# Two-phase 31-tap convolution with three half-length filters, two parts per tile, in a DeltaNet/Conformer layer

## The chip, the cores and the metric

The program runs on one core of one Trainium2 chip. The metric is the device time of one execution, in microseconds (us). The engines are named as the profile names them: PE (TensorE matmul), PEld (its weight load), DVE (VectorE), ACT (ScalarE), POOL (GpSimd), SP (SyncE, which here only issues DMAs). Each engine takes its instructions in the order in which they were written into its queue; they wait for each other through semaphores.

## The reference

One layer over 128 context and 2048 latent tokens of width 1024, in float32:

```python
h = rmsnorm(x, g_pre_mix) * (1.0 + scale_m) + shift_m
proj = h @ w_in
qkv, z, ab, glu = jnp.split(proj, [3 * D_A, 4 * D_A, 4 * D_A + 4 * N_HEADS_A], axis=-1)
qkv = jax.nn.silu(dwconv1d(qkv, conv_qkv))          # 5 taps
...                                                  # gated DeltaNet on q, k, v; z gates its output o
glu_a, glu_b = jnp.split(glu, 2, axis=-1)
u = glu_a * jax.nn.sigmoid(glu_b)
u = dwconv1d(u, conv_cf) + b_conv_cf                 # 31 taps, depthwise, 512 channels
u = jax.nn.silu(layernorm(u, ln_cf_g, ln_cf_b))
mix = jnp.concatenate([o, u], axis=-1) @ w_out
x = x + gate_m * rmsnorm(mix, g_post_mix)
...                                                  # gated MLP with a 3x3 convolution in its gate branch
```

`dwconv1d` pads with zeros on both sides; context and latent tokens are convolved separately.

## The kernel before

The program has four stages: the projections with everything that hangs on them (to about 775 us), the DeltaNet chains (to about 1100), the output projection `mix` (to about 1313), and the MLP. The change lies in the first, and by one edit in the third.

**Stage 1.** The products with `w_in` are 24 jobs in a fixed order on PE. A job multiplies 128 columns of `w_in` with all 2176 tokens, in five token blocks (512, 512, 512, 320, 320), as three fp32r products (high and low halves of both sides; L361 to L363), 120 products in all. The order of the jobs that matter here is: glu0, ab (the small decay and beta projection), k1, z0, k0, glu1, z1, glu2, k2, z2, glu3, k3, z3, q0, v1, q1, v0, v3, v2, q2, q3. A glu job computes two projections, 240 products.

- `do_glu(m, ...)`: ACT takes a sigmoid in PSUM (L385), copies the other half into the big buffer `ub` (L390), DVE multiplies (L391). `ub` holds 128 channels and, along its length, 2048 latent and 128 context tokens with zeros between them.
- `do_cf(m, ub, half)`: the 31-tap convolution of tile m, in two token halves of 1024 and 1167 columns. `conv` makes the first tap on ACT (L372) and the other 30 on DVE, one SCALAR_TENSOR_TENSOR each, in place in `acc` (L375). The result is stored to `d_uc` in DRAM (L399).
- `do_conv5`: the 5-tap convolutions of q, k and v (one tap on ACT, four on DVE, the same lines), a Silu (L417) and what follows: for k small products of keys with keys on PE (`pkk`, L446), copied by ACT into `ar` and stored to `d_a` (L448, L449); for q and k the norms (`pqs`, L456, L460); for v transposes (`pt`, L434).
- `do_scalars`: decay and beta of each token: a row of constants `rb` is loaded (L562), DVE and ACT compute from it and from `abT` (L570 to L598), PE sums with six small products (L600 to L602).
- LayerNorm of the convolution's output: `d_uc` is read back, transposed on PE (`ptl`, L534), its statistics taken on DVE (L535), and later applied.

The big buffers A, B and C (`bigA`, `bigB`, `bigC` in the rows) carry `ub` and the inputs of the 5-tap convolutions in turn, B also the temporaries of `do_scalars`, later the winit and inversion work. The pool `ac` has two accumulators, `sm` four buffers for its shared tag "sm", among them `ar` and the rows `gr` that `do_scalars` stores. The order on every engine is decided when the program is built, by a scheduler that plays the program on a timeline of its own costs; `high_priority` pulls the evacuations of PSUM ahead.

**Stage 3.** `mix_in` loads the 128 tokens of a chunk (`mx`, 8 groups of 128 columns: 0 to 3 are o, 4 to 7 are u), splits them into a high and a low half (`mH` on ACT, L1133; `mL` on POOL, L1134), and PE multiplies them with the halves of `w_out`.

Of the kernel before, what the change touches and what calls it, by code (L numbers as in the profile page):

```python
# [47 lines left out]
def hybrid_step_kernel(ctx, tc, x, wmod, pv, rows, win, wab, wout, wup, wdown, s0, cst,  # L48
# [34 lines left out]
    def pvs(n):  # L83
        a, b = PV[n]
        return pvt[:, a:b]
# [165 lines left out]
    with ExitStack() as s1:  # L251
# [23 lines left out]
        def load_w(m):  # L275
            wt = wp.tile([P, KD, P], F32, name="wt", tag="ws", bufs=1)
            nc.sync.dma_start(wt[:], win[m])
            wr = wp.tile([P, 2, KD, P], F32R, name="wr", tag="wr")
            with tc.high_priority():
                nc.scalar.copy(wr[:, 0], wt[:])  # L280
                nc.gpsimd.tensor_tensor(wr[:, 1], wt[:], wr[:, 0].bitcast(F32), ALU.subtract)
            return wr
# [88 lines left out]
        def conv(dst, src, o, n, w, taps, bias=None):  # L371
            nc.scalar.activation(dst, src[:, o:o + n], AF.Identity, scale=w[:, 0:1],  # L372
                                 bias=0.0 if bias is None else bias)
            for t in range(1, taps):
                nc.vector.scalar_tensor_tensor(dst, src[:, o + t:o + t + n], w[:, t:t + 1], dst, ALU.mult, ALU.add)  # L375

        def do_glu(m, sl, w=None):
            ub = slot(sl, [P, 2224])
            for a, b in ((0, 15), (2063, 2078), (2206, 2221)):
                nc.gpsimd.memset(ub[:, a:b], 0.0)  # L380
            wb, wa = w or (load_w(20 + m), load_w(16 + m))
            for bi in range(len(BLOCKS)):
                s, n, pb = mm_block(wb, bi)
                with tc.high_priority():
                    nc.scalar.activation(pb[:, 0:n], pb[:, 0:n], AF.Sigmoid)  # L385
                s, n, ps = mm_block(wa, bi)
                with tc.high_priority():
                    for a, ln, off, pr in pieces(s, n):
                        o = (2078 if pr else 15) + off
                        nc.scalar.copy(ub[:, o:o + ln], ps[:, a:a + ln])  # L390
                        nc.vector.tensor_tensor(ub[:, o:o + ln], ub[:, o:o + ln], pb[:, a:a + ln], ALU.mult)  # L391
            return ub

        def do_cf(m, ub, half):
            acc = ac.tile([P, 1168], F32, name="acc", tag="acc")
            w = pvs("ccf")[:, 31 * m:31 * m + 31]
            n = 1167 if half else 1024
            conv(acc[:, 0:n], ub, 1024 * half, n, w, 31, pvs("bcf")[:, m:m + 1])
            nc.sync.dma_start(d_uc[8 * half:8 * half + 8, :, m, :].rearrange("c p t -> p c t"),  # L399
                              acc[:, 0:1024].rearrange("p (c t) -> p c t", t=P))  # L400
            if half:
                nc.sync.dma_start(d_uc[16, :, m, :], acc[:, 1039:1167])

        def do_conv5(m, sl, post):
            cb = slot(sl, [P, 2224])
            for a, b in ((0, 2), (2050, 2052), (2180, 2182)):
                nc.gpsimd.memset(cb[:, a:b], 0.0)
            for s, n, ps in project(m):
                with tc.high_priority():
                    for a, ln, off, pr in pieces(s, n):  # L410
                        o = (2052 if pr else 2) + off
                        nc.scalar.copy(cb[:, o:o + ln], ps[:, a:a + ln])  # L412
            for half in range(2):
                acc = ac.tile([P, 1168], F32, name="acc", tag="acc")
                n = 1154 if half else 1024
                conv(acc[:, 0:n], cb, 1024 * half, n, pvs("cqkv")[:, 5 * m:5 * m + 5], 5)
                nc.scalar.activation(acc[:, 0:n], acc[:, 0:n], AF.Silu)  # L417
                post(acc, half, cb)
# [139 lines left out]
            nc.sync.dma_start(d_mix[c, :, 4:8, :], uv)  # L558

        def do_scalars(tt, abT):  # L560
            rb = sm.tile([P, 16], F32, name="rb", tag="rb", bufs=1)
            nc.sync.dma_start(rb[:], rows.to_broadcast([P, 16]))  # L562
            N16 = [P, NT, 16]
            trs = tt[:, 1428:1940].rearrange("p (a t) -> p a t", t=P)
            nc.sync.dma_start(trs, cst[:, 1:5, :])
# [20 lines left out]
            nc.vector.tensor_tensor(t3, t3, t4, ALU.add)  # L586
            nc.vector.tensor_scalar(t0, t0, 0.0, None, ALU.max)
            nc.vector.tensor_tensor(t3, t3, t0, ALU.add)
            ea = sm.tile([P, 8], F32, name="ea", tag="ea", bufs=1)
            nc.scalar.activation(ea[:], rb[:, 0:8], AF.Exp)  # L590
            nc.vector.tensor_scalar(ea[:], ea[:], -1.0, None, ALU.mult)
            NTH = NT * H
            for d in range(2):
                fl = lambda t: t[:, d].rearrange("p c h -> p (c h)")
# [133 lines left out]

        def inv(b, eng):
            invs[b] = invert(b, eng, ltb[:, 0:1056], prod,  # L730
                             lambda: ac.tile([P, 1168], F32, name="xo", tag="acc")[:, 0:1024])
            run(invs[b], 32)

        def inv_end(b):
# [365 lines left out]
    with ExitStack() as s3:  # L1100
# [9 lines left out]
        def mix_in(c):  # L1110
            on = wi.tile([P, H, P], F32, name="on3", tag="on3")
            nc.sync.dma_start(on[:], d_o[c].rearrange("p (h t) -> p h t", h=H))
            zt = wi.tile([P, H, P], F32, name="zt", tag="zt")
            nc.sync.dma_start(zt[:], d_z[c])
            mx = wi.tile([P, KD, P], F32, name="mx", tag="mx")
            nc.sync.dma_start(mx[:, 4:8], d_mix[c, :, 4:8])
            sc = s3p.tile([P, H], F32, name="sc", tag="sc", bufs=2)
            for h in range(H):
                junk = s3p.tile([P, P], BF16, name="junk0", tag="junk0", bufs=4)
                nc.scalar.activation(junk[:], on[:, h], AF.Square, accum_out=sc[:, h:h + 1])  # L1120
            nc.vector.tensor_tensor(sc[:], sc[:], rq2[:, c], ALU.mult)
            last_a = nc.scalar.activation(sc[:], sc[:], AF.Sqrt, scale=1.0 / P, bias=epsb[:]).ins
            nc.vector.reciprocal(sc[:], sc[:])
            last_v = nc.vector.tensor_tensor(sc[:], sc[:], rq[:, c], ALU.mult).ins
            nc.gpsimd.tensor_tensor(on[:], on[:], sc[:].unsqueeze(2).to_broadcast([P, H, P]), ALU.mult)
            po = ptr.tile([P, H, P], F32, name="pto", tag="tr")
            for h in range(H):
                nc.tensor.transpose(po[:, h], on[:, h], ident[:])
            f = lambda t: t.rearrange("p h i -> p (h i)")
            nc.vector.scalar_tensor_tensor(f(mx[:, 0:4]), f(po[:]), pvs("gon"), f(zt[:]), ALU.mult, ALU.mult)  # L1130
            mH = wh.tile([P, KD, P], F32R, name="mH", tag="mH", bufs=2)
            mL = wi.tile([P, KD, P], F32R, name="mL", tag="mL", bufs=2)
            nc.scalar.copy(mH[:], mx[:])  # L1133
            nc.gpsimd.tensor_tensor(mL[:], mx[:], mH[:].bitcast(F32), ALU.subtract)  # L1134
            return mH, mL, last_a, last_v

        def mix_mm(c, mH, mL):
# [78 lines left out]
    if True:  # L1216
# [7 lines left out]
        def taps(j):  # L1224
            return pvf[:, 9 * j:9 * j + 9], pvf[:, 198 + j:199 + j]
# [395 lines left out]
```

## Time and profile before

| | |
|---|---|
| median of 3 runs | 2793.51 us (2789.07 to 2797.16) |
| the profiled execution's own time | 2791.89 us |
| its span in the profile | 2790.1 us |
| mean granted clock of PE over the span | 0.972 |

The profile is of one execution. Its span runs from the first to the last instruction; 1.8 us of the time lie outside it. PE is busy 2654.8 us of the span, DVE 1907.2. A share of the whole span is a mean over four stages with different limits, so the rows below are taken by stage. [...]

### The profile page before, as it was taken

The numbers are of one execution on the slowest core, as the hardware profiler recorded it, in microseconds if no ns is written. First come the engines' busy times: TensorE is split into PE (matmuls) and PEld (weight loads), VectorE is DVE, ScalarE is ACT, GpSimd is POOL, SyncE is SP. The second block draws the span as 40 slices with busy tenths as digits, with TensorE's granted clock in tenths as the row PEclk, the third lists the DMA queues.
The fourth block names the chain that finished last, engine by engine and source line by source line (L and its number), as shares of the span: only waits on it lengthen the run. The fifth ranks groups of instructions, "written<-read, shape, count | busy, mean of one in ns | idle before, by whom it ended". The sixth has DMA issues, their size and how long they took to land.

```text
span 2790.1 us, 41624 instructions
## 1 busy us (share of the span) xinstructions
PE 2654.8 (95%) x15309; PEld 2237.8 (80%) x15309; DVE 1907.2 (68%) x2840; ACT 1153.1 (41%) x2421; POOL 789.9 (28%) x851
## 2 busy tenths in 40 slices
PE   7999999979888998999899999999999999999998
PEld 4888888767778887888788888888888878888887
DVE  3898999885657785444687777887888873225343
ACT  5423132355656666666544444432222232224221
POOL 2211011166335683222666666500000000000000
PEclk9999999989969999999999999999999999999999
DMA  7024531576597565665777777888777754236453
GB/s 275 20 72 119 151 109 43 104 190 134 154 279 195 141 227 207 219 231 184 256 278 266 265 271 262 279 263 255 235 232 222 230 184 134 94 104 211 165 173 119
DMA packets 426712, 526.79 MB, mean 189 GB/s; under 512 B 144790, under 2 KB 301964, under 8 KB 426252
## 3 DMA queue, kind: packets, MB, share of 16 engines
q1 hardware_dynamic: 406380, 506.30, 57.5%
q10 hardware_dynamic: 20128, 17.83, 1.9%
q8 instruction: 121, 1.98, 0.3%
q14 instruction: 83, 0.68, 0.1%
HBM read 342.13 MB, written 181.90 MB: 188 GB/s over the span
## 4 chain that ended last, share of the span: by engine, by line
PE 61%; DMA 5%; DVE 4%; ACT 3%; SPq 3%; POOL 2%; issue 2%; ACTq 0%; DVEq 0%; POOLq 0%
PE ps L1318 10%; PE ps L1320 10%; PE ps L1319 10%; PE ps L1147 7%; PE ps L1486 6%; PE ps L1484 6%; PE ps L1485 6%; PE psc L1232 2%; SPq L166 1%; DVE dm L819 1%; PE p L938 1%; PE p L945 1%; DMA dm<-d_g 1%; DMA d_mix<-bigB 1%; PE p L957 1%
## 5 line engine op out<-in xcount | busy, mean ns | idle before, releaser
L1377 DVE SCALAR_TENSOR_TENSOR pa<-gb,pvf,pa 128x512 f32<-128x512 f32 (+1 forms) x704 | 491.0, 733 | 65.3 <-ACT pa L1375 62.5
L1318 PE MATMUL ps<-T,wr 128*128 128x512 f32 x1232 | 480.5, 391 | 0.1
L1319 PE MATMUL ps<-T,wr 128*128 128x512 f32 x1232 | 479.9, 389 | 0.0
L1320 PE MATMUL ps<-T,wr 128*128 128x512 f32 x1232 | 479.0, 390 | 0.6 <-POOL wr L1246 0.6
L361 PE MATMUL ps<-hH,wr 128*128 128x512 f32 (+1 forms) x960 | 349.7, 369 | 6.6 <-ACT bigA L412 3.8
L362 PE MATMUL ps<-hL,wr 128*128 128x512 f32 (+1 forms) x960 | 352.4, 367 | 0.0
L363 PE MATMUL ps<-hH,wr 128*128 128x512 f32 (+1 forms) x960 | 350.6, 366 | 0.0
L1484 PE MATMUL ps<-wd,yr 128*128 128x512 f32 x748 | 292.5, 391 | 6.1 <-ACT yr L1480 5.5
L1486 PE MATMUL ps<-wd,yr 128*128 128x512 f32 x748 | 292.1, 391 | 0.4 <-DVE yr L1481 0.4
L1485 PE MATMUL ps<-wd,yr 128*128 128x512 f32 x748 | 292.1, 391 | 0.0
L1318 PEld LDWEIGHTS ps<-T,wr 128*128 128x128 f32 x1232 | 231.4, 188 | 49.2 <-issue 0.8
L1320 PEld LDWEIGHTS ps<-T,wr 128*128 128x128 f32 x1232 | 231.4, 188 | 49.1 <-POOL wr L1246 1.1
L1319 PEld LDWEIGHTS ps<-T,wr 128*128 128x128 f32 x1232 | 231.4, 188 | 47.4
L375 DVE SCALAR_TENSOR_TENSOR acc<-bigA,pvt,acc 128x1024 f32<-128x1024 f32 (+2 forms) x168 | 252.3, 1502 | 13.2 <-ACT acc L372 9.2
L361 PEld LDWEIGHTS ps<-hH,wr 128*128 128x128 f32 x960 | 184.0, 193 | 33.5 <-ACT bigA L412 4.2
L1481 DVE TENSOR_TENSOR yr<-yt,yr 128x1408 fp32r<-128x1408 f32 x68 | 110.5, 1625 | 143.4 <-ACT yr L1480 143.3
L363 PEld LDWEIGHTS ps<-hH,wr 128*128 128x128 f32 x960 | 185.4, 193 | 25.4 <-issue 3.0
L362 PEld LDWEIGHTS ps<-hL,wr 128*128 128x128 f32 x960 | 185.3, 193 | 24.0 <-issue 1.6
L1351 POOL TENSOR_TENSOR up<-up,x 128x512 f32<-128x512 f32 x44 | 57.3, 1302 | 413.2 <-ACT pa L1383 217.9
L375 DVE SCALAR_TENSOR_TENSOR acc<-bigC,pvt,acc 128x1024 f32<-128x1024 f32 (+2 forms) x108 | 156.6, 1461 | 24.9 <-DMA bigB<-d_uc 15.5
L1484 PEld LDWEIGHTS ps<-wd,yr 128*128 128x128 f32 x748 | 141.0, 188 | 36.6 <-ACT yr L1480 6.5
L1486 PEld LDWEIGHTS ps<-wd,yr 128*128 128x128 f32 x748 | 141.0, 188 | 30.7 <-DVE yr L1481 1.4
(360 smaller groups left out, 4571.2 us busy)
## 6 DMA issues: line engine op xcount, KB each, us to landing
d_w<-wr SPq DMA_DIRECT2D x154, 512.0 KB
wr<-d_w SPq DMA_DIRECT2D x154, 512.0 KB
yt<-d_y SPq DMA_DIRECT2D x68, 704.0 KB
raw<-in_wup_dram SPq DMA_DIRECT2D x60, 512.0 KB
xt<-in_x_dram SPq DMA_DIRECT2D x34, 512.0 KB
wmt<-in_wmod_dram SPq DMA_DIRECT2D x24, 512.0 KB
wt<-in_win_dram SPq DMA_DIRECT2D x24, 512.0 KB
wmt<-in_wmod_dram SPq DMA_DIRECT2D x48, 256.0 KB
```

The source lines that it names most:

```text
L361: nc.tensor.matmul(ps[:, 0:n], wr[:, 0, k], hH[bi][:, k], start=(k == 0), stop=False)
L362: nc.tensor.matmul(ps[:, 0:n], wr[:, 0, k], hL[bi][:, k], start=False, stop=False)
L363: nc.tensor.matmul(ps[:, 0:n], wr[:, 1, k], hH[bi][:, k], start=False, stop=(k == KD - 1))
L375: nc.vector.scalar_tensor_tensor(dst, src[:, o + t:o + t + n], w[:, t:t + 1], dst, ALU.mult, ALU.add)
L1147: nc.tensor.matmul(pss[hf][:], a[:, k], w[k][:, 512 * hf:512 * hf + 512], start=(w is woH and a is mH and k == KD - 1), stop=(w is woL and ...
L1318: nc.tensor.matmul(ps[:], h, T[i][:, 0, k], start=(first and k == 0), stop=False, skip_group_check=True)
L1319: nc.tensor.matmul(ps[:], h, T[i][:, 1, k], start=False, stop=False, skip_group_check=True)
L1320: nc.tensor.matmul(ps[:], l, T[i][:, 0, k], start=False, stop=(k == HK - 1), skip_group_check=True)
L1377: nc.vector.scalar_tensor_tensor(rows(a), src, w[:, t:t + 1], rows(a), ALU.mult, ALU.add)
L1484: nc.tensor.matmul(ps[:], yr[:, 0, i], wd[:, 0], start=(q == 0 and i == 0), stop=False)
L1485: nc.tensor.matmul(ps[:], yr[:, 0, i], wd[:, 1], start=False, stop=False)
L1486: nc.tensor.matmul(ps[:], yr[:, 1, i], wd[:, 0], start=False, stop=(q == 1 and i == HN - 1))
```

## The change

The convolution is done by phases. With e the even and o the odd tokens, an even output is A(e) + B(o) and an odd output is D(e + o) - A(e shifted) - B(o), where A has the 16 even taps, B the 15 odd taps and D the 16 sums of neighbouring taps. So three filters of half length replace two phases of full length.

- `do_glu` writes `ub` de-interleaved: one half of the buffer for each parity. ACT and DVE read PSUM with a stride of two elements for it (L393, L394 in the changed file).
- `do_cf` works in two parts of 512 and 584 tokens per parity. ACT makes two first taps (L412, L413), DVE 15 taps of A and 14 of B, which take turns, then the sum of the parities in place (L418), the two outputs' start (L420, L421), and 16 steps of D (L422, and 15 in L399): 48 instructions of half length where 30 of full length stood. The D output stays in `ub`, and each part is stored as two blocks with runs of 64 elements (256 bytes) where runs of 128 (512 bytes) stood. POOL saves and restores 15 columns around the sum of the first part (L417, L425).
- Within each chunk of 128 tokens the order in `d_uc` is now all even, then all odd tokens. `mix_in` undoes it: `mH` and `mL` are made in two pieces each, the second with a strided read of `mx`.
- `wc`, the sums of taps, is a new small buffer. To keep the memory, `rb` leaves its own buffer and takes one of the four of the tag "sm", and `ea` becomes a part of it. The accumulators have 1169 columns for 1168; the weight buffers stay two.

```diff
@@ -376,8 +376,9 @@
         def do_glu(m, sl, w=None):
             ub = slot(sl, [P, 2224])
-            for a, b in ((0, 15), (2063, 2078), (2206, 2221)):
+            for a, b in ((0, 7), (1031, 1039), (1103, 1119), (2143, 2151), (2215, 2224)):
+            uv = ub.rearrange("p (h i) -> p h i", h=2)
...
                     for a, ln, off, pr in pieces(s, n):
-                        o = (2078 if pr else 15) + off
-                        nc.scalar.copy(ub[:, o:o + ln], ps[:, a:a + ln])
-                        nc.vector.tensor_tensor(ub[:, o:o + ln], ub[:, o:o + ln], pb[:, a:a + ln], ALU.mult)
+                        o = (1039 if pr else 7) + off // 2
+                        u = uv[:, :, o:o + ln // 2]
+                        ev = lambda t: t[:, a:a + ln].rearrange("p (i h) -> p h i", h=2)
+                        nc.scalar.copy(u, ev(ps))
+                        nc.vector.tensor_tensor(u, u, ev(pb), ALU.mult)
+        def taps(dst, src, w, n, t0):
+            for t in range(t0, n):
+                nc.vector.scalar_tensor_tensor(dst, src(t), w(t), dst, ALU.mult, ALU.add)
+
+        wc = sm.tile([P, 32], F32, name="wc", tag="wc", bufs=1)
+
         def do_cf(m, ub, half):
-            acc = ac.tile([P, 1168], F32, name="acc", tag="acc")
             w = pvs("ccf")[:, 31 * m:31 * m + 31]
-            n = 1167 if half else 1024
-            conv(acc[:, 0:n], ub, 1024 * half, n, w, 31, pvs("bcf")[:, m:m + 1])
-            nc.sync.dma_start(d_uc[8 * half:8 * half + 8, :, m, :].rearrange("c p t -> p c t"),
-                              acc[:, 0:1024].rearrange("p (c t) -> p c t", t=P))
-            if half:
-                nc.sync.dma_start(d_uc[16, :, m, :], acc[:, 1039:1167])
+            i0, n = (512, 584) if half else (0, 512)
+            xo, xe = ub[:, i0:1111], ub[:, 1111 + i0:2223]
+            if not half:
+                nc.vector.tensor_tensor(wc[:, 0:15], w[:, 0:30:2], w[:, 1:30:2], ALU.add)
+                nc.vector.tensor_copy(wc[:, 15:16], w[:, 30:31])
+            acc = ac.tile([P, 1169], F32, name="acc", tag="acc")
+            A, B = acc[:, 0:n + 1], acc[:, n + 1:2 * n + 1]
+            nc.scalar.activation(A, xe[:, 0:n + 1], AF.Identity, scale=w[:, 0:1])
+            nc.scalar.activation(B, xo[:, 0:n], AF.Identity, scale=w[:, 1:2])
+            taps(A, lambda t: xe[:, t:t + n + 1], lambda t: w[:, 2 * t:2 * t + 1], 16, 1)
+            taps(B, lambda t: xo[:, t:t + n], lambda t: w[:, 2 * t + 1:2 * t + 2], 15, 1)
+            if not half:
+                nc.gpsimd.tensor_copy(wc[:, 16:31], xo[:, n:n + 15])
+            nc.vector.tensor_tensor(xo[:, 0:n + 15], xo[:, 0:n + 15], xe[:, 1:n + 16], ALU.add)
+            bias, D_, Ae = pvs("bcf")[:, m:m + 1], xe[:, 0:n], A[:, 0:n]
+            nc.vector.scalar_tensor_tensor(D_, A[:, 1:n + 1], bias, B, ALU.subtract, ALU.add)
+            nc.vector.scalar_tensor_tensor(Ae, Ae, bias, B, ALU.add, ALU.add)
+            nc.vector.scalar_tensor_tensor(D_, xo[:, 0:n], wc[:, 0:1], D_, ALU.mult, ALU.subtract)
+            taps(D_, lambda t: xo[:, t:t + n], lambda t: wc[:, t:t + 1], 16, 1)
+            if not half:
+                nc.gpsimd.tensor_copy(xo[:, n:n + 15], wc[:, 16:31])
+            for h, y in enumerate((Ae, D_)):
+                nc.sync.dma_start(d_uc[8 * half:8 * half + 8, :, m, 64 * h:64 * h + 64].rearrange("c p t -> p c t"),
+                                  y[:, 0:512].rearrange("p (c t) -> p c t", t=64))
+                if half:
+                    nc.sync.dma_start(d_uc[16, :, m, 64 * h:64 * h + 64], y[:, 520:584])
 
...
         def do_scalars(tt, abT):
-            rb = sm.tile([P, 16], F32, name="rb", tag="rb", bufs=1)
-            nc.sync.dma_start(rb[:], rows.to_broadcast([P, 16]))
+            rb = sm.tile([P, 24], F32, name="rb", tag="sm", bufs=4)
+            nc.sync.dma_start(rb[:, 0:16], rows.to_broadcast([P, 16]))
...
-            ea = sm.tile([P, 8], F32, name="ea", tag="ea", bufs=1)
-            nc.scalar.activation(ea[:], rb[:, 0:8], AF.Exp)
-            nc.vector.tensor_scalar(ea[:], ea[:], -1.0, None, ALU.mult)
+            ea = rb[:, 16:24]
+            nc.scalar.activation(ea, rb[:, 0:8], AF.Exp)
+            nc.vector.tensor_scalar(ea, ea, -1.0, None, ALU.mult)
...
-            nc.scalar.copy(mH[:], mx[:])
-            nc.gpsimd.tensor_tensor(mL[:], mx[:], mH[:].bitcast(F32), ALU.subtract)
+            for sl, v in ((slice(0, 4), lambda t: t), (slice(4, 8), lambda t: t.rearrange("p k (h i) -> p k i h", h=2))):
+                o = (lambda t: t) if sl.start == 0 else (lambda t: t.rearrange("p k (i h) -> p k i h", h=2))
+                nc.scalar.copy(o(mH[:, sl]), v(mx[:, sl]))
+                nc.gpsimd.tensor_tensor(o(mL[:, sl]), v(mx[:, sl]), o(mH[:, sl].bitcast(F32)), ALU.subtract)
```

In the order of instructions the edit moves work at three places. Buffers carry their program names; `gdt` is the decay of each token and head, and the rows with `hH` and `hL` are the products of the projection jobs.

PE, the end of job k0 and the start of glu1, before:

```order
L363 MATMUL ps<-hH_548,wr 128x320
L600 MATMUL ps<-gdt,bigB 128x68
L601 MATMUL ps<-gdt,bigB 128x68
L602 MATMUL ps<-gdt,ones 128x68
L600 MATMUL ps<-gdt,bigB 128x68
L601 MATMUL ps<-gdt,bigB 128x68
L602 MATMUL ps<-gdt,ones 128x68
L361 MATMUL ps<-hH_136,wr 128x512
```

The same place after the change:

```order
L363 MATMUL ps<-hH_548,wr 128x320
L474 MATMUL pkk<-acc 128x128 x17
L628 MATMUL ps<-gdt,bigB 128x68
L629 MATMUL ps<-gdt,bigB 128x68
L630 MATMUL ps<-gdt,ones 128x68
L628 MATMUL ps<-gdt,bigB 128x68
L629 MATMUL ps<-gdt,bigB 128x68
L630 MATMUL ps<-gdt,ones 128x68
L361 MATMUL ps<-hH_136,wr 128x512
```

The six products of `do_scalars` stand between k0 and glu1 in both. New ahead of them are all 17 `pkk` products of k0 itself; before, these stood inside glu1, 15, 95 and 113 products later.

SP, the load of `rb`, before (it is among the first DMAs of the program):

```order
L277 DMA wt<-in_win_dram 128x1024
L676 DMA mk_725<-in_cst_dram 32x32 x4
L562 DMA rb<-in_rows_dram 128x16
L185 DMA wmt<-in_wmod_dram 128x2x512 x8
```

After (`ar` is what ACT copies out of k0's `pkk`, `wmt` the next weights of the modulation):

```order
L477 DMA d_a<-ar 128x4x128 x2
L477 DMA d_a<-ar 128x128
L590 DMA rb<-in_rows_dram 128x16
L643 DMA d_g<-gr 68x128
L185 DMA wmt<-in_wmod_dram 128x4x128
```

The load of `rb` has moved from the start of the program to behind the last of k0's five `ar` stores, since it takes a buffer of the tag that they use.

DVE, the first steps of `do_scalars`, before (in the taps of glu0's convolution, ahead of k1's):

```order
L526 COPY abT<-pt 128x272
L375 SCALAR_TENSOR_TENSOR acc<-bigA,pvt,acc 128x1024
L570 TENSOR_TENSOR bigB<-abT,rb 128x17x8
L572 TENSOR_SCALAR bigB<-abT 128x17x8
L375 SCALAR_TENSOR_TENSOR acc<-bigA,pvt,acc 128x1024
L573 TENSOR_SCALAR bigB<-bigB 128x272
```

After (the four taps are the second half of k0's convolution; `rb` waits for ACT's Exp of it, L618):

```order
L399 SCALAR_TENSOR_TENSOR bigA<-bigA,wc 128x584 x6
L408 TENSOR_TENSOR wc<-pvt 128x15
L409 COPY wc<-pvt 128x1
L375 SCALAR_TENSOR_TENSOR acc<-bigC,pvt,acc 128x1154 x4
L598 TENSOR_TENSOR bigB<-abT,rb 128x17x8
L619 TENSOR_SCALAR rb<-rb 128x8
L601 TENSOR_SCALAR bigB<-bigB 128x272
L602 TENSOR_TENSOR bigB<-bigB 128x272
```

The chain of `do_scalars` has moved as a whole behind k0's last taps, and no other work stands between its steps. Later, on PE, the norms of q0 (`pqs`) stand behind the products 17 and 88 of job v1, where they stood behind 41 and 96, and the first `ptl` behind 96 of v1, where it stood behind 28 of q1.

## Rows read from the trace of the kernel before

**Rows 1.** Busy time of each engine by stretch: us, busy (instructions) of each, granted clock, DMA.

```profile
core 0: us, PE busy (x) PEld busy (x) DVE busy (x) ACT busy (x) POOL busy (x), PEclk, DMA share, GB/s
300.00:400.00 100.00, 99.97 (x691) 84.47 (x690) 93.89 (x76) 23.96 (x35) 9.54 (x7) 1.00 0.44 125
507.00:532.00 25.00, 23.92 (x125) 20.75 (x124) 21.18 (x25) 10.38 (x17) 2.43 (x1) 1.00 0.55 80
532.00:576.00 44.00, 29.36 (x141) 23.97 (x140) 42.31 (x36) 19.94 (x28) 15.03 (x11) 0.81 0.59 123
576.00:775.00 199.00, 172.12 (x895) 147.22 (x894) 129.42 (x145) 110.94 (x223) 107.58 (x166) 0.94 0.65 166
1107.00:1313.00 206.00, 205.41 (x996) 170.83 (x995) 96.78 (x180) 128.45 (x406) 52.32 (x30) 1.00 0.65 218
```

**Rows 2.** Waits of PE, 500 to 795 us: waited for, us in total, times, longest.

```profile
PE pqs L456 <- ACT bigA L453: 10.9, 2, 8.5
PE pt L434 <- ACT vt L480: 9.5, 4, 4.0
PE ptl L534 <- DMA bigB<-d_uc: 7.6, 4, 5.8
PE ps L361 <- ACT bigA L412: 3.8, 1, 3.8
```

**Rows 3.** The same view of PE, 100 to 500 us.

```profile
PE pkk L446 <- ACT acc L417: 3.2, 1, 3.2
```

**Rows 4.** Timeline of DVE (start, us, what, count): one chain of taps, then two in turns.

```profile
249.72 7.89 DVE L375 SCALAR_TENSOR_TENSOR acc<-bigC,pvt,acc 128x1024 f32<-128x1024 f32 x6
...
373.84 1.28 DVE L375 SCALAR_TENSOR_TENSOR acc<-bigA,pvt,acc 128x1024 f32<-128x1024 f32 x1
375.03 1.28 DVE L375 SCALAR_TENSOR_TENSOR acc<-bigC,pvt,acc 128x1024 f32<-128x1024 f32 x1
```

**Rows 5.** All instructions of line 1377 in the MLP: ns min/median/max, first and last, forms.

```profile
L1377 DVE SCALAR_TENSOR_TENSOR pa<-gb,pvf,pa x704: 672/748/757, 1375.7 to 2308.7; 128x512 f32<-128x512 f32 x175, 128x448 f32<-128x448 f32 x1
```

**Rows 6.** The same view of line 391, glu0 and glu2.

```profile
L391 DVE TENSOR_TENSOR bigA<-bigA,ps x12: 276/583/686, 63.6 to 355.9; 128x512 f32<-128x512 f32 x6, 128x320 f32<-128x320 f32 x2, 128x192 f32<-128x192 f32 x2, 128x128 f32<-128x128 f32 x2
```

**Rows 7.** A group of DVE by form, 100 to 600 us: xcount | busy us, mean ns | idle before.

```profile
L375 DVE SCALAR_TENSOR_TENSOR acc<-bigA,pvt,acc 128x1024 f32<-128x1024 f32 x72 | 103.1, 1432 | 1.5 <-ACT acc L372 0.2
```

**Rows 8.** Timeline of PE: last product of k0, the six small products, first of glu1.

```profile
209.47 0.31 PE L363 MATMUL ps<-hH,wr 128*128 128x320 f32 x1
209.61 0.34 PE L600 MATMUL ps<-gdt,bigB 128*128 128x68 f32 x2
...
210.87 0.48 PE L361 MATMUL ps<-hH,wr 128*128 128x512 f32 x1
```

**Rows 9.** Timeline of PE, DVE and ACT behind job k2, second half: last product, taps, Silu.

```profile
380.04 0.31 PE L363 MATMUL ps<-hH,wr 128*128 128x320 f32 x1
...
384.90 6.58 DVE L375 SCALAR_TENSOR_TENSOR acc<-bigC,pvt,acc 128x1154 f32<-128x1154 f32 x4 [3.80 <-ACT acc L372]
...
391.51 1.18 ACT L417 ACTIVATE acc<-acc 128x1154 f32<-128x1154 f32 x1 [2.03 <-DVE acc L375]
```

**Rows 10.** Timeline of SP and DVE: the last small loads of skT, and their first reader.

```profile
511.66 1.80 SPq L504 DMA_DIRECT2D skT<-d_a  x2
...
516.71 0.20 DVE L505 TENSOR_SCALAR skT<-skT 128x68 f32<-128x68 f32 x1 [2.13 <-DMA skT<-d_a]
```

**Rows 11.** Timeline of ACT and DVE: steps of do_scalars.

```profile
134.88 1.28 ACT L575 ACT_TABLE_LOAD   x1 [10.26 <-DVE bigB L574]
...
142.96 1.85 DVE L583 RECIPROCAL bigB<-bigB 128x272 f32<-128x272 f32 x1
147.02 0.44 DVE L584 TENSOR_TENSOR bigB<-bigB 128x272 f32<-128x272 f32 x1
```

**Rows 12.** Timeline of DVE: last tap of glu3's convolution (bigB), then q0's (bigA).

```profile
573.39 1.42 DVE L375 SCALAR_TENSOR_TENSOR acc<-bigB,pvt,acc 128x1167 f32<-128x1167 f32 x1
```

**Rows 13.** All instructions that write or read the tile mH, on ACT.

```profile
L1133 ACT CAST mH<-mx x17: 1030/1077/1118, 1098.1 to 1293.2; 128x1024 fp32r<-128x1024 f32 x17
```

More of the change, by code (lines that the diff above doesn't have):

```diff
@@ L413, in do_conv5 @@
             for half in range(2):
-                acc = ac.tile([P, 1168], F32, name="acc", tag="acc")
+                acc = ac.tile([P, 1169], F32, name="acc", tag="acc")
                 n = 1154 if half else 1024
@@ L730, in inv @@
             invs[b] = invert(b, eng, ltb[:, 0:1056], prod,
-                             lambda: ac.tile([P, 1168], F32, name="xo", tag="acc")[:, 0:1024])
+                             lambda: ac.tile([P, 1169], F32, name="xo", tag="acc")[:, 0:1024])
             run(invs[b], 32)
```

## Prediction

> **What bounds the kernel now.** I read the busy time by stretch first, then the waits of PE, then the timelines around them. From 300 to 400 us PE is busy all the time, and DVE 94 of 100 us [rows 1]. So PE sets the pace there, and DVE follows closely: whatever DVE saves in that stretch is not time by itself. The picture turns at job v1, 532 to 576 us: PE is busy 29 of 44 us at a granted clock of 0.81, DVE 42 of 44, while the job before, q0, took the usual 25 us with PE busy 24 [rows 1]. Same number of products, 19 us more. The waits name the causes: 10.9 us for the squares of q0's convolution (`pqs`), 3.8 us for an evacuation behind them on ACT [rows 2]. DVE there works off the last taps of glu3's convolution in turns with q0's, and ends the former at 574.8 [rows 12]. From 576 to 775 PE idles another 27 of 199 us [rows 1], for the `d_uc` loads (7.6) and for v tiles (9.5) [rows 2]. Stage 3 has PE busy 205.4 of 206 us [rows 1]. Time can thus be won where PE waits for DVE's convolutions, some 42 us of idle time from 532 to 775, and lost wherever PE gets a new wait in the stretch where it is the bound.
>
> **The taps.** A chain of 1024-column taps alone runs at 7.89 / 6 = 1.315 us a tap, and two chains in turns at 1.19 [rows 4]; the latter takes 1.28 us by its duration, and the same operation over 512 columns 0.748 [rows 5]. That is a slope of 0.53 us for 512 columns, so I price a tap in turns at 1.19 - 0.53 = 0.66 us for 512 columns and 0.66 + 72 x 0.00104 = 0.735 for 584; alone 0.125 more, 0.79 and 0.86. For 1167 it is 1.34 and 1.465. Before, a tile costs 30 x (1.19 + 1.34) = 75.9 us in turns and 83.4 alone. After, 29 taps of A and B in turns, four steps around them and 15 of D alone: 33 x 0.66 + 15 x 0.79 = 33.6, and 33 x 0.735 + 15 x 0.86 = 37.2, together 70.8. A tile saves 5 to 12.6 us of DVE; I take 10, because most taps of glu1 to glu3 run alone. The mean of 1.43 us over 72 taps [rows 7] holds disturbances that I leave out on both sides.
>
> [...]
>
> **The strided PSUM reads.** A tile has six multiplications at L391, 0.58 us the median [rows 6], some 3.1 us. No row has a stride of two on DVE. Below, nothing is added; above, each doubles, 3 us. I take 1. So DVE gains 7 to 9 us a tile.
>
> **The new wait between k0 and glu1.** This is the largest term. Before, the six small products of `do_scalars` follow k0 with no gap, and glu1 starts at 210.87 [rows 8]; its chain had run long before, around 135 us inside glu0's taps [rows 11]. After, that chain begins when `rb` is there, and `rb` is loaded behind k0's last `ar` store, while PE cannot pass the small products: all 240 products of glu1 are queued behind them. I walk it. k0 ends 4 to 5 us sooner than at 209.6, since the 3.2 us for `pkk` [rows 3] at 178 us fall away (DVE has less in front of k1's taps): 205. From k2's last product to the first tap of its second half 4.9 us pass, then 6.6 for four taps, and a Silu of 1.2 [rows 9]: 205 + 12.7 = 217.7. DVE is free for these taps by then, at about 208 by my tap prices. The last nine `pkk`, priced like the six small products, 1.3 us [rows 8], and three copies on ACT of 1152 columns together, priced like the Silu, 1.2: 220. A small load has landed 5.0 us after the start of its last two issues, 1.8 us long [rows 10]: 3.5 for one, 223.5. Exp of `rb` with its table load of 1.28, then thirteen steps of DVE: twelve of at most 0.44 and a reciprocal of 1.85, and two ACT steps of 0.4 with one more table load [rows 11]: 1.6 + 6 + 2 = 9.6, 233. The small products, 1.3 us: glu1 starts at 234. That is 23 us late. Off it go 2 us for the 17 `pkk` that are done in the wait, and on it 2 for half clock at the restart, as the lower clock in rows of v1 follows its waits [rows 1]. Ends: 18, if the steps of DVE cost half of 0.44 and the load lands in 2; 27, if DVE reaches the taps 4 us later. I take 23, with the gain at 178 already inside. From glu1 to q0 PE is the bound, so nothing of it is recovered before v1.
>
> **v1.** The pause also lets DVE run dry and start glu1 level with PE, and DVE then saves 7 to 9 us on each of glu1 to glu3; not all of it counts, since DVE cannot run ahead of PE. What surely counts is glu3's own convolution, whose second half ends 574.8 before. By the prices it has 10 us less in it, and q0's taps between come earlier by the same. The two `pqs` waits were 10.9 with a longest of 8.5 [rows 2]. But they now stand 24 and 8 products sooner in v1, 5 and 2 us. The first stays about as it was, the second falls by 8; with the evacuation's 3.8 behind it and the lower clock, 19 us lost become 7. I take -12; nothing below -19, nothing above -4.
>
> **576 to 775.** The first `ptl` now waits for `d_uc` inside v1; its 5.8 us stay or go, +1 as the middle. Inversions and LayerNorm start earlier against PE, but v tiles still hang on latency through ACT: 27 us idle fall by 0 to 10; -4.
>
> **What lies beside other work.** Eight extra first taps on ACT, which is busy 24 of 100 us [rows 1]; the POOL copies of 15 columns; and the stores' halved runs, which end long before their reader except the last. Stage 3: `mH` costs 1.08 us a chunk [rows 13]; the strided half may double, +0.5 on ACT and a like share on POOL, 17 times. ACT is busy 128 and POOL 52 of 206 us while PE never waits [rows 1], so this hides but for the first chunk: +0.5. Without that cover it would be 17 x 1 = 17 us.
>
> **The sum.** 23 - 12 + 1 - 4 + 0.5 = +8.5 against the profiled execution's 2791.9, which stands 1.6 below the median of 2793.5: 2800. Ends: 18 - 19 - 10 = -11, 27 - 4 + 3 = +26.
>
> **The rivals.** *Faster*: the taps' gain is what counts. The wait at k0 comes at its lower end, and all that PE waited for from 532 to 775 was DVE's lag, so that v1 gives back 19 and the rest 14: 18 - 33 = -15, 2777. For it speaks DVE's 42 of 44 us in v1; against it that `pqs` and `ptl` were moved forward by about as much as DVE gains, and that the waits for v tiles name ACT. *No difference*: the chain is shorter than my walk, 12 to 15, because ACT and SP get to the load of `rb` sooner and DVE's steps overlap, while v1 and the tail go as summed: -2, 2790. Against it: the steps all depend on each other and none of the rows has them faster. *Slower by more*: v1 keeps its stall because it hangs on q0's own evacuation, squares and `pqs`, which move with PE: +23 - 2 = +21, 2813. It decides if PE still waits over 8 us for `pqs`. For it: ACT is named in both waits [rows 2].
>
> **How the numbers follow.** The summed case 0.55, with its own range 2791 to 2808; slower by more 0.17; no difference 0.15; faster 0.13. Within 0.3%, 8.4 us, is what a measurement here can tell from no change. The summed case lies half on either side of that bound, so: faster 0.14, same 0.44, slower 0.42. Leaving out the outer half of the two far cases the range is 2781 to 2814.
>
> **What would show it.** PE idle 20 to 25 us ahead of the first L628, released by DVE's last steps of `do_scalars`, and DVE busy with only these steps in that time; no wait for `pkk` at 178; taps of 0.75 us in duration at 512 columns; waits for `pqs` under 8 us in v1, and a PE that stays at 1.00 from glu1 to z3. The prediction is wrong if the wait at L628 is under 12 us, if v1 takes 40 us again, or if PE gets idle time in stage 3.

## The result, and the profile after

The changed kernel takes 2808.51 us (median of 6 runs, 2805.31 to 2815.92), the kernel before in the same runs 2791.29 (2782.78 to 2797.16). The ratio is 1.0083, with a 95% interval of 1.0061 to 1.0104: slower by 0.83%, which is 23 us of 2791; the two medians lie 17 us apart. The profiled execution is one of 2805.31, 13.4 us above that of before. The forecast was +8.5 with a range to 2814, and it gave "slower" a chance of 0.42 and "same" 0.44: right in direction, and too small by half to two thirds.

The waits of PE in the changed kernel, from 100 to 520 us and then from 500 to 850 (waited for, us in total, times, longest):

```profile
PE ps L628 <- DVE gdt L624: 14.6, 1, 14.6
PE pkk L474 <- ACT acc L445: 9.9, 1, 9.9
...
PE pt L462 <- ACT acc L445: 13.0, 2, 11.4
PE ptl L562 <- DMA bigB<-d_uc: 7.0, 5, 4.0
...
PE pqs L484 <- ACT bigA L481: 4.3, 1, 4.3
```

The first two are new and together one pause of 24.5 us: PE stands between k0 and glu1, first for k0's own `pkk`, then for the last steps of `do_scalars`. Against [rows 2], the waits in v1 for q0's `pqs` fell from 10.9 to 4.3 us, and a wait of 11.4 us for a v tile is new. Two further waits for `pqs`, of 2.7 and 2.5 us, come later, in v0 and q3, and are new as well.

Busy time by stretch, of the changed kernel (us, busy of PE, PEld, DVE, ACT, POOL, granted clock, DMA). The stretches are q0, v1, the rest of stage 1, and stage 3; the last three lie in the pause and behind it:

```profile
530.00:556.00 26.00, 24.46 (x127) 21.23 (x127) 18.92 (x32) 11.67 (x17) 3.94 (x1) 1.00 0.51 75
556.00:591.00 35.00, 28.59 (x145) 23.06 (x144) 21.66 (x31) 17.31 (x25) 8.83 (x10) 0.90 0.69 151
591.00:790.00 199.00, 167.60 (x890) 143.41 (x888) 129.86 (x147) 116.62 (x232) 118.01 (x167) 0.94 0.62 167
1118.00:1326.00 208.00, 207.79 (x993) 172.40 (x992) 95.61 (x182) 135.17 (x424) 64.36 (x50) 0.99 0.68 228
...
219.00:224.00 5.00, 4.00 (x18) 3.71 (x18) 0.00 (x0) 1.36 (x3) 0.00 (x0) 0.50 0.59 170
237.00:241.00 4.00, 3.41 (x14) 3.32 (x15) 1.18 (x7) 0.93 (x6) 0.27 (x5) 0.50 0.00 0
241.00:250.00 9.00, 9.00 (x33) 7.07 (x33) 0.18 (x1) 2.39 (x4) 0.00 (x0) 0.78 0.14 37
```

Against [rows 1], v1 is 35 us long for 44, and DVE, which was busy 42 of 44 us there, is busy 22 of 35: most of its lag is gone (e4 below shortens v1 further). The rest of stage 1 is as long as before. Stage 3 has no idle time of PE. The granted clock is given as a share of PE's full speed: it is 1.00 over q0, and 0.50 in both stretches of the pause, behind PE's waits of 9.9 and 14.6 us.

What the jobs gain and lose is best seen by the start of each job's first product, worked out from the trace (us, with the first product of the program set to 11.8 in each; e1 and e2 are experiments below):

```
             before   after      e1      e2
k1            128.3   131.1   127.7   130.2
k0            186.3   183.4   180.1   184.9
glu1          210.9   240.0   206.7   248.1
z1            269.0   298.6   264.3   306.4
glu2          296.8   322.8   289.9   331.0
z3            478.0   503.3   472.7   516.9
q0            507.8   530.6   499.9   545.5
v1            532.5   555.8   525.1   571.1
q1            576.3   591.4   562.9   612.7
v0            612.0   627.6   598.5   653.0
v3            649.0   672.7   642.3   690.5
v2            681.5   698.1   667.6   715.9
end of q3     775.3   789.6   761.9   808.3
mix          1099.3  1116.8  1076.0  1130.8
```

The column "after" minus "before": +29.1 at glu1, +26.0 at glu2, +22.8 at q0, +23.3 at v1, +15.1 at q1, +23.7 at v3, +14.3 at the end of stage 1. Between glu1 and v1 the shift so falls by 5.8 us. glu1 and z1 together are 3.1 shorter, since k0's 17 `pkk` have been done in the pause; z3 is 2.5 shorter, since two of its waits before are gone (PE of the kernel before, 500 to 795 us):

```profile
PE ps L361 <- ACT zs L488: 1.1, 1, 1.1
PE pkk L446 <- ACT acc L417: 0.9, 1, 0.9
```

The pause itself, by the timelines of the engines that pass it on (PE, DVE, ACT and SP of the changed kernel):

```profile
206.98 1.95 PE L474 MATMUL pkk<-acc 128*128 128x128 f32 x16
218.80 4.21 PE L474 MATMUL pkk<-acc 128*128 128x128 f32 x18 [9.87 <-ACT acc L445]
237.59 0.70 PE L628 MATMUL ps<-gdt,bigB 128*128 128x68 f32 x2 [14.58 <-DVE gdt L624]
...
211.68 5.86 DVE L375 SCALAR_TENSOR_TENSOR acc<-bigC,pvt,acc 128x1154 f32<-128x1154 f32 x4
227.47 0.30 DVE L598 TENSOR_TENSOR bigB<-abT,rb 128x136 f32<-128x136 f32 x1 [9.92 <-DMA rb<-in_rows_dram]
237.30 0.23 DVE L624 TENSOR_TENSOR gdt<-bigB,rb 128x68 f32<-128x68 f32 x1
...
217.58 1.17 ACT L445 ACTIVATE acc<-acc 128x1154 f32<-128x1154 f32 x1 [6.84 <-DVE acc L375]
222.66 0.77 ACT L476 ACTIVATE ar<-pkk 128x512 f32<-128x512 f32 x2 [1.16 <-PE pkk L474]
228.82 0.21 ACT L618 ACTIVATE rb<-rb 128x8 f32<-128x8 f32 x1
...
221.53 2.67 SPq L477 DMA_DIRECT2D d_a<-ar  x3
224.29 0.40 SPq L590 DMA_DIRECT2D rb<-in_rows_dram  x1
```

Read from the top of DVE: k0's last taps end at 217.5, the Silu at 218.75, PE's `pkk` and ACT's copies at 223.4; SP has issued the three stores at 224.2 and only then loads `rb`; DVE has stood 9.9 us when it lands, and goes through its steps to 237.5; PE does the small products.

The taps, by form (xcount | busy us, mean ns), one group of taps in turns and one alone (start, us, count), and the new multiplications (ns min/median/max):

```profile
L399 DVE SCALAR_TENSOR_TENSOR bigA<-bigA,wc 128x512 f32<-128x512 f32 x30 | 26.8, 892 | 1.0
...
L399 DVE SCALAR_TENSOR_TENSOR acc<-bigA,pvt,acc 128x512 f32<-128x512 f32 x28 | 22.9, 819 | 0.0
...
181.77 5.26 DVE L399 SCALAR_TENSOR_TENSOR acc<-bigA,pvt,acc 128x585 f32<-128x585 f32 x7
192.23 5.14 DVE L399 SCALAR_TENSOR_TENSOR bigA<-bigA,wc 128x584 f32<-128x584 f32 x6
...
L394 DVE TENSOR_TENSOR bigA<-bigA,ps x12: 272/581/689, 64.6 to 381.9; 128x512 f32<-128x512 f32 x6, 128x320 f32<-128x320 f32 x2, 128x192 f32<-128x192 f32 x2, 128x128 f32<-128x128 f32 x2
```

Half a tap costs 0.82 to 0.89 us on average against 1.43 for a whole one [rows 7], and the strided multiplications cost 0.581 against 0.583 at the median [rows 6]. In stage 1 DVE is busy 574.0 us for 618.6, some 11 us less a tile where the prediction had 10 for the taps. The convolution does save what was said; it is what else moved that decides.

### The profile page after: what moved, and what is told of

Same layout as the page of the kernel before. It is cut to its first block, busy times and chain, and to the rows that moved or that the text cites. A ratio compares the mean times of both kernels' runs of the same rounds, so it can differ in the third digit from the quotient of the medians.

```text
span 2803.3 us, 41888 instructions
## 1 busy us (share of the span) xinstructions
PE 2649.6 (95%) x15309; PEld 2236.3 (80%) x15309; DVE 1851.7 (66%) x2992; ACT 1155.0 (41%) x2444; POOL 801.0 (29%) x884
## 4 chain that ended last, share of the span: by engine, by line
PE 73%; DVE 9%; DMA 7%; ACT 4%; SPq 3%; issue 2%; POOL 2%; ACTq 0%; DVEq 0%; POOLq 0%
PE ps L1350 9%; PE ps L1348 9%; PE ps L1349 9%; PE ps L1177 7%; PE ps L1516 6%; PE ps L1514 6%; PE ps L1515 6%; PE ps L361 4%; PE ps L362 4%; PE ps L363 4%; PE psc L1262 2%; DVE dm L847 1%; DVE pa L1407 1%; DMA dm<-d_g 1%; PE psr L190 1%
## 5 line engine op out<-in xcount | busy, mean ns | idle before, releaser
L363 PEld LDWEIGHTS ps<-hH,wr 128*128 128x128 f32 x960 | 183.8, 191 | 24.5 <-issue 2.0
L1514 PEld LDWEIGHTS ps<-wd,yr 128*128 128x128 f32 x748 | 140.8, 188 | 37.1 <-ACT yr L1510 6.5
L1516 PEld LDWEIGHTS ps<-wd,yr 128*128 128x128 f32 x748 | 140.6, 188 | 30.6 <-DVE yr L1511 1.6
L1515 PEld LDWEIGHTS ps<-wd,yr 128*128 128x128 f32 x748 | 140.8, 188 | 29.1
L1510 ACT CAST yr<-yt 128x1408 fp32r<-128x1408 f32 x68 | 93.1, 1369 | 167.9 <-PE ps L1516 91.1
```

The lines of the kernel that those rows point to most:

```text
L363: nc.tensor.matmul(ps[:, 0:n], wr[:, 1, k], hH[bi][:, k], start=False, stop=(k == KD - 1))
L1514: nc.tensor.matmul(ps[:], yr[:, 0, i], wd[:, 0], start=(q == 0 and i == 0), stop=False)
L1515: nc.tensor.matmul(ps[:], yr[:, 0, i], wd[:, 1], start=False, stop=False)
L1516: nc.tensor.matmul(ps[:], yr[:, 1, i], wd[:, 0], start=False, stop=(q == 1 and i == HN - 1))
```

## The experiments

Times are medians, ratios those to the kernel before in the same runs. Stage 1 is the end of q3 as in the table.

**e1, the constants in a buffer of their own.** Against the changed kernel:

```diff
-        wc = sm.tile([P, 32], F32, name="wc", tag="wc", bufs=1)
+        wc = sm.tile([P, 16], F32, name="wc", tag="wc", bufs=1)
-                nc.gpsimd.tensor_copy(wc[:, 16:31], xo[:, n:n + 15])
+                nc.gpsimd.tensor_copy(acc[:, 1100:1115], xo[:, n:n + 15])
-                nc.gpsimd.tensor_copy(xo[:, n:n + 15], wc[:, 16:31])
+                nc.gpsimd.tensor_copy(xo[:, n:n + 15], acc[:, 1100:1115])
-            rb = sm.tile([P, 24], F32, name="rb", tag="sm", bufs=4)
+            rb = sm.tile([P, 16], F32, name="rb", tag="rb", bufs=1)
-            ea = rb[:, 16:24]
+            ea = rb[:, 0:8]
```

> The changed kernel, but the constants of do_scalars have their own buffer again and are loaded at the start of the program (room for them is won elsewhere: the 15 saved columns go to unused columns of the accumulator, and the Exp of the constants is made in place). The six small products stand between k0 and glu1 with nothing ahead of them, as in the kernel before. Theory 1, the load of rb behind k0's stores is the whole loss and the convolution itself gains a little: PE's wait ahead of L628 is under 1 us, glu1 starts within 3 us of 211, v1 takes 35 us for 44, and the time is 2780 to 2788, 5 to 10 below before and some 22 below the changed kernel. Theory 2, the convolution itself is worth nothing on the path, since stalls only move from v1 to the jobs behind it: the wait is gone and the time is within 3 us of before. Theory 3, the convolution's other edits lose too: 2798 or more.

Measured: 2781.63 us (12 runs), ratio 0.9984 (0.9965 to 1.0004), 27 us below the changed kernel. The time lies in theory 1's bracket, but before stood at 2785.1 in these runs, so it is 3.5 below by the medians and not 5 to 10. glu1 starts at 206.7, v1 takes 37.8 us, and stage 1 ends at 761.9. The waits of PE from 100 to 500 us in e1 are all of these:

```profile
PE ps L549 <- DVE wabr L543: 1.2, 1, 1.2
PE psr L190 <- DMA wmt<-in_wmod_dram: 1.1, 2, 0.8
PE pgr L640 <- DVE gdt L634: 0.3, 1, 0.3
```

The pause is gone with this edit alone. Against before the convolution then gains 13 us of stage 1 by this profile: by the table 7.4 are won ahead of v1, most of it by k0, where the wait of [rows 3] for `pkk` is gone, 6.0 in v1, and nothing behind it. The whole time is lower by only 4.5 by the ratio, and cannot be told from no change at 95%.

**e2, only the constants moved.** Against the kernel before:

```diff
-            rb = sm.tile([P, 16], F32, name="rb", tag="rb", bufs=1)
-            nc.sync.dma_start(rb[:], rows.to_broadcast([P, 16]))
+            rb = sm.tile([P, 24], F32, name="rb", tag="sm", bufs=4)
+            nc.sync.dma_start(rb[:, 0:16], rows.to_broadcast([P, 16]))
...
-            ea = sm.tile([P, 8], F32, name="ea", tag="ea", bufs=1)
+            ea = rb[:, 16:24]
```

> The kernel before with only one part of the change: rb takes a buffer of the tag sm, ea is a part of it. The 31-tap convolution is the old one. Its order has k0's 17 pkk and the small products ahead of glu1 just as the changed kernel has. Theory 1: this alone makes PE wait 22 to 30 us ahead of glu1, part of which comes back at v1, since DVE catches up in the pause and only v1's 15 us of idle time can return: 2803 to 2815. Theory 2, that DVE's lag at v1 is as large as the pause, so that all but a little comes back: 2791 to 2798.

Measured: 2820.07 us (6 runs), ratio 1.0129 (1.0107 to 1.0151); stage 1 ends at 808.3. The two waits of the pause, in e2:

```profile
PE pkk L446 <- ACT acc L417: 15.8, 2, 15.1
PE ps L600 <- DVE gdt L596: 15.0, 1, 15.0
```

More than either theory said. With the old convolution, DVE reaches k0's last taps later, the pause is 30 us, and v1 still takes 41.6 us: the pause does not free DVE as I had thought. The four kernels make a square of stage 1's end: 775.3 and 808.3 with the old convolution, 761.9 and 789.6 with the new one. So the constants cost 33 and 28 us, and the convolution saves 13 and 19. Whether `rb` could take the shared tag and still be loaded early, by another place in the order, no run tested.

**e3, stage 3 without the undoing of the order.** Against e1, `mH` and `mL` made in one contiguous step each, as before:

> As e1_rb_own, but mH and mL are made in one contiguous step each, as before; the tokens of the second half of the columns so stay in the even-odd order, which the reference does not have. Theory 1, the strided halves hide under PE in stage 3: the time is that of e1_rb_own within 2 us, and the first product of stage 3 comes at most 1 us sooner. Rival: POOL's or ACT's longer split is late for PE, and the time falls by 4 us or more.

Measured: 2777.56 us (12 runs), ratio 0.9974 (0.9953 to 0.9995); its interval overlaps that of e1. By the medians it is 4.1 us below e1, as the rival asked. But from the first product of mix to the last are 210.5 us for e1's 209.6, and stage 1 ends at 763.2. So the edit in stage 3 is hidden, and the 4 us are not seen in that stage. Whether the first product comes sooner could not be seen, since the second stage scatters by far more (below).

**e4, a shorter D.** Against e1:

```diff
-            taps(D_, lambda t: xo[:, t:t + n], lambda t: wc[:, t:t + 1], 16, 1)
+            taps(D_, lambda t: xo[:, t:t + n], lambda t: wc[:, t:t + 1], 8, 1)
```

> As e1_rb_own, but D has 8 taps for 16, so the odd outputs lack half their taps; DVE loses some 13 us of work per tile, a further saving of the size of the change's own. Theory 1, PE sets the pace from glu1 to z3 and only v1 and the jobs behind can shrink: 0 to 6 us below e1_rb_own. Rival, that DVE's convolution sets the end of stage 1: 10 us or more below it.

Measured: 2770.87 us (12 runs), ratio 0.9950 (0.9933 to 0.9967); stage 1 ends at 756.5. The job v1 took 43.8 us before, 37.8 in e1 and 32.8 here: it follows DVE. But q1 takes 41.5 us here and 35.6 in e1. Some 50 us less work on DVE (4 tiles of 13) end stage 1 by 5.4 us sooner, which is theory 1's size. The medians differ by 10.8, which is the rival's; the profiles show half of it in stage 1, and the rest is not explained.

**e5 and e6, the queue behind the inversion.** In e1, and alike in the changed kernel, this chain leads to the wait for v3's tile, by the timelines of POOL, SP and DVE of e1:

```profile
683.61 2.39 POOL L281 TENSOR_TENSOR wr<-wt,wr 128x1024 fp32r<-128x1024 f32 x1
...
686.03 0.33 SPq L277 DMA_DIRECT2D wt<-in_win_dram  x1
686.46 0.38 SPq L579 DMA_DIRECT2D bigB<-d_uc  x1
...
690.58 0.84 DVE L582 TENSOR_TENSOR bigB<-bigB,rw 128x512 f32<-128x512 f32 x1 [9.82 <-DMA bigB<-d_uc]
```

And the longest wait of PE in the same stretch of e1:

```profile
PE pt L462 <- ACT acc L445: 11.8, 1, 11.8
```

A step for the next weights stands on POOL behind the inversion; SP waits for it with a weight load, the load of `d_uc` stands behind that, DVE waits 9.8 us for this load with v3's taps behind it. Against e1, low halves of the weights go to DVE:

```diff
-                nc.gpsimd.tensor_tensor(wr[:, 1], wt[:], wr[:, 0].bitcast(F32), ALU.subtract)
+                (nc.vector if m in LATE else nc.gpsimd).tensor_tensor(wr[:, 1], wt[:], wr[:, 0].bitcast(F32), ALU.subtract)
```

> As e1_rb_own, but the low halves of the weights of the q and v jobs are made by DVE, not by POOL, where they are queued behind steps of the inversion. In e1_rb_own such a step on POOL is late, SP waits with the next weight load, a load of d_uc is queued behind that on SP, DVE waits for it with the taps of v3 queued behind, and PE waits 11.8 us for v3. Theory 1, this queue is where the convolution's gain at v1 is given back: the wait of PE for v3 falls below 4 us, stage 1 ends 5 to 10 us sooner than in e1_rb_own (762 us), and the time falls by as much, to 2771 to 2777. Rival: v3 is late for its own reasons and the DVE work added (8 steps of some 1.2 us) makes it later: stage 1 ends at 760 or later.

Measured: 2779.84 us (10 runs), ratio 0.9978 (0.9965 to 0.9990), stage 1 ends at 766.7, where the rival had 760 or later. It does not answer the question: `LATE` held the jobs of k and v (4 to 11), and the step in question, q2's, stayed on POOL. PE's longest wait there is 13.1 us. So with `LATE = (2, 3)`:

> As e1_rb_own, but the low halves of the weights of q2 and q3, the two steps on POOL that e1_rb_own makes at 684 and 709 us behind the inversion, are made by DVE. (e5_late_dve moved those of the k and v jobs by mistake and left these two on POOL.) Theory 1, the queue POOL, SP, DVE is where v1's gain is given back: SP's load of q3's weights comes 10 us or more sooner than in e1_rb_own, the wait of PE for v3 of 11.8 us falls below 4, stage 1 ends at 752 to 758 for 762, and the time is 5 to 10 below e1_rb_own. Rival: v3 stays late, since its taps wait for other loads too: stage 1 ends at 760 or later and the time is the same within 3 us.

Measured: 2776.80 us (12 runs), ratio 0.9964 (0.9946 to 0.9981), stage 1 ends at 765.2. SP issues the weight load at 677.2 for 686.0, 8.9 us sooner, and PE still waits 9.4 us in one piece:

```profile
PE pt L464 <- ACT vt L510: 12.4, 3, 9.4
```

The theory falls: this queue was not the only one. By the timelines of POOL and ACT of e6, another instruction on POOL stands behind the inversion there, the one that writes the zeros at the borders of the next input of a 5-tap convolution (L437):

```profile
702.43 0.17 POOL L437 MEMSET bigA<- 128x2 f32 x3
...
702.56 1.15 ACT L374 ACTIVATE acc<-bigA,pvt 128x1024 f32<-128x1024 f32 x1 [9.30 <-POOL bigA L437]
...
705.62 2.16 ACT L510 ACTIVATE vt<-pt,isk 128x128 f32<-128x128 f32 x8
```

ACT waits 9.3 us with its first tap for these zeros, and the copies of v3's transposes (`vt`), for which PE waits, stand behind that tap. This is read from one trace; no run moved these zeros to see what it would be worth. e6 is the fastest kernel here that leaves nothing out, 0.36% below before and clear of no change, but not shown to be below e1.

**e7, the same edit on the kernel before.**

> The kernel before, with only the two low halves of q2's and q3's weights on DVE as in e6_q23_dve. Theory 1: there POOL's late step was less in the way (before, PE waits 4.5, 3.2 and 4.0 us in the jobs v2 and q2), so it gains 0 to 5 us, less than in e6_q23_dve. Rival: the queue costs the kernel before as much, so it gains the same and the convolution has no part in it.

Measured: 2801.58 us (6 runs), ratio 1.0053 (1.0036 to 1.0070). Stage 1 ends at 775.1 as before, so neither theory holds there: the edit gains nothing in stage 1, and the 15 us are lost behind it. In the profile 8 of 11 us lie in the second stage; the reason no run here tells.

**Three more profiles**, to see what of a difference is scatter.

> The kernel before, profiled once more, to see how far a stage differs between two executions of one program. If the scatter of the times lies in the second stage (from the last projection to the first product of mix), stage 1 ends within 2 us of 775, while the second stage differs from its 324 us by up to 10.

> e1_rb_own, profiled once more. If stage 1's gain of 13 us is real and the scatter lies behind it: stage 1 ends within 2 us of 762, and the second stage takes more than the 314 us of the first profile. If stage 1 itself scatters: its end is off by 5 us or more.

> The changed kernel, profiled once more: the wait ahead of L628 within 1 us of 14.6 and that for pkk within 1 of 9.9, stage 1 ending within 2 us of 790, the second stage between 314 and 336.

Measured: stage 1 ended at 771.9 (before), 762.7 (e1) and 792.6 (changed): within 3.4, 0.8 and 3.0 us of the first profiles, where 2 had been expected. The two waits of the pause came again at 14.8 and 9.9 us, and glu1 started at 240.6 for 240.0. The second stage, from the end of q3 to the first product of mix, took 317.7, 316.0 and 326.5 us, and in e3 336.0. By the two profiles of before, two of after and two of e1, stage 1 ends at 773.6, 791.1 and 762.3 in the mean: +17.5 for the change, -11.3 for the convolution without the moved constants.

## Why the prediction was wrong

**What failed is the gain that the sum put at v1 and behind it**: -12, and -4 with +1 for `ptl`, -15 together. The runs show -9.0 by the table, and -6.8 in the mean of two profiles of each kernel. The shift that reaches v1 is +23.3 (24.3 in the mean of two), where the sum had 23. So these two gains were sized too high, and of the 6.3 us by which stage 1 missed the sum (14.3 for 8), 3.8 lie in v1, 2.2 behind it and 0.3 ahead of it.

**The pause between k0 and glu1.** That this term fits is luck in part. By the walk glu1 starts at 234, and it starts at 240; and where the prediction says that nothing of the pause is recovered before v1, 5.8 us are. The order of the links was as told; nearly each was a little longer. The Silu ended at 218.75 for 217.7: DVE was not free at 208 but at 211.7, and the start of k0 lay 3 us lower only, not 4 to 5, since k1 began 2.8 later. The copies ended at 223.4 for 220, a lag of 2.3 more: the last nine `pkk`, 18 instructions in the trace, took 4.2 us at a granted clock of 0.50, for 1.3 in the walk. The first 16 took 1.95 at 1.00, so the price was too low without the clock too. `rb` landed at 227.4 for 223.5: behind the copies, SP still had 0.9 us of the stores' issue in front of it, which I had left out. The steps on DVE and ACT took 10.1 us for 9.6. The six small products took 2.6 us at 0.50, for 1.3 at 1.00 before. Together 6 us. The sum's 2 us for half clock at the restart stand beside 0.78 in the 9 us behind the pause; in the kernel before, the clock was 0.50 from 564 to 572 us, among v1's waits. e1 and e2 show that this move, and nothing else in the change, makes the pause.

**v1.** Predicted -12, measured -8.2 (43.8 to 35.6; 43.7 to 37.6 in the second profiles). The direction, and that DVE's lag is behind it, hold: e1 and e4 shorten v1 with DVE's work. PE's idle time in v1 fell from 14.6 to 6.4 us: the first wait for `pqs` is gone, the second is 4.3 for 8.5 where I had it fall by 8. But PE is busy there some 29 us in both, though I had counted on the clock to come back: it rose from 0.81 to 0.90 only, and 8 of the `ptl` instructions now stand in v1. Part of the gain is then given back further on: v0 takes 45.1 us for 37.0, while v3 takes 25.4 for 32.5 and v2 38.7 for 36.5.

**576 to 775.** Predicted -4 and +1 for `ptl`; from the start of q1 to the end of q3 are 198.2 us for 199.0, -0.8. The wait for `d_uc` stayed, 7.0 for 7.6 us, and a wait for v3 took the place of two or three shorter ones. In e1 this stretch takes 199.0 us and in e4, with the least work on DVE, 200.4. That the tail hangs on latency and not on DVE was right, and makes the gain I still put there wrong.

**The rival "faster"** priced all that PE waited for from 532 to 775 as DVE's lag. Even e4, with far less work on DVE, ends stage 1 only 19 us sooner than before; the rival's conditions do not occur. "No difference" needed a pause of 12 to 15 us, and it was 24.5. "Slower by more" decided by a wait of over 8 us for `pqs`, and there is none in v1; the time came near its 2813 by way of the smaller gains and of what lies behind stage 1. Of the signs of being wrong none came: the wait at L628 was 14.6 us, v1 took 35.6, and stage 3 has no idle PE.

**The small terms** held: the strided PSUM reads of DVE show no price, 0.581 us at the median for 0.583 contiguous (I took 1 us a tile); stage 3 is hidden; taps alone and in turns ran at 0.86 and 0.75 us a piece for 584 columns, by the groups of 6 and 7 taps (5.14 and 5.26 us), for 0.86 and 0.735.

**From the profile to the median.** In the profile the change costs 14.3 us of stage 1 and 13.4 of the whole; by the ratio 0.83%, 23 us. Two profiles each give 17.5 for stage 1. The rest lies within the scatter of the second stage, as does the distance between e1's 11 us in stage 1 and its 4.5 in the time. That the second stage takes more in one kernel than in another is not shown. But the executions of e1 were granted less: 0.971 in the median of its 12, for 0.974 in the 29 of before.

## What to carry to other kernels

When a tile moves into a shared, rotating tag to save memory, follow its load in the order of the DMA queue: it now waits for the release of the buffer it is given and for all that is issued ahead, and everything that is computed from it moves along. Here the load of a tile of 96 bytes a partition was issued at 224.3 us, behind three stores, and this made the difference between 0.83% slower and a time that can't be told from before. Work saved on DVE, which followed PE, was worth only what PE waited for it: the changed kernel has 44.6 us less of it in stage 1, and e1, with the same convolution, ends that stage 11.3 us sooner. Part of the wait turned up some jobs later: in e4 v1 is 5.0 us shorter than in e1, and q1 5.9 longer.

## What the runs showed of the hardware

The second stage, many short products with waits between them, took 314 to 336 us over the twelve profiles, with 3508 to 3511 products in the eight where they were counted. In these eight the length went with the granted clock: the three shortest (314, 316, 318 us) had 0.93, 0.93 and 0.91, the two of the changed kernel (327 and 326) 0.89, the two longest (333, 336) 0.86. The two ends are e1 and e3, whose first two stages are the same program. e1:

```profile
763.00:1076.00 313.00, 284.02 (x3509) 262.60 (x3509) 209.16 (x476) 201.17 (x613) 187.13 (x299) 0.93 0.68 204
```

and the same stage of e3:

```profile
764.00:1099.00 335.00, 303.10 (x3508) 280.53 (x3508) 218.71 (x479) 202.52 (x614) 184.23 (x299) 0.86 0.65 192
```

PE is busy 19 us longer at 0.86 than at 0.93, which is most of the 22 us between them. The kernel before was at 0.91 in its 324 us. What made the clock differ is not shown. The whole times follow it too: of e1's 12 executions the fastest, 2765.8 us, was granted 0.976, the slowest, 2792.0, 0.967. So an effect of 10 us in stage 1 is plain in the trace of one execution, where that stage came again within 3.4 us, and hard to see in the time of a dozen.
